# Two raw weight sets, split subtractions, powers by columns and later pages in a two-layer decoder step

## The chip, the cores and the metric

The kernel runs on one core of a Trainium2 chip. A core has TensorE (matrix products, PE in the profile, with its weight loads as PEld), VectorE (DVE), ScalarE (ACT), GpSimd (POOL) and SyncE (SP), which here only issues DMAs. The engines run their own instruction queues in order and wait for one another by semaphores. The metric is the device time of one execution in microseconds (us); lower is better.

## The reference

One inference step of a decoder with two layers, for a prompt of 512 tokens and eight samples of eight new tokens each (576 columns in all), in float32:

```python
# layer 0
h = modulate(x, norm_a, shift, scale)
qkv, z, beta_in, a_in = split(h @ w_in_a)
q, k, v = split(silu(causal_conv(qkv)))
o, s = gated_delta_rule(l2_normalize(q), l2_normalize(k), v, g, beta, s0)
x = x + gate * ((rms_norm(o) * silu(z)) @ w_out_a)
# shared keys and values
k_new, v_new = split(modulate(x, norm_kv, ...) @ w_kv)   # k: rms_norm, partial rotary
# layer 1
q, z = split(modulate(x, norm_b, ...) @ w_in_b)          # q: rms_norm, partial rotary
p = softmax(q1 @ k1) - lam * softmax(q2 @ k2)            # samples: 1024 cached positions too
x = x + gate * ((rms_norm(p @ v) * silu(z)) @ w_out_b)
```

The samples' cached keys and values stand in 128-position pages, found by a page table. Outputs are the new x, the recurrent states, the convolution states and the new keys and values.

## The kernel before

**Products in two parts.** A weight matrix is cut into sets of 1024 x 128 (512 KB). TensorE multiplies in the type fp32r, which keeps fewer bits than float32. So a set w is held as an upper part hi (w rounded to fp32r) and a lower part lo = w - hi, and the activations likewise as hhi and hlo. A product is the sum of hi x hhi, hi x hlo and lo x hhi. The 576 columns are treated in two halves of 288 (HT); a set takes 2 x 24 matmuls.

**How a set is loaded.** In the first layer (`first_parts`, `negatives`, `second_parts`, lines 919 to 943) GpSimd issues a DMA from `wall` that rounds into hi (`new_set`, L906), ScalarE writes lo = -hi (`negative`, L911), and GpSimd issues a second DMA that adds w to lo (`second_part`, L916). Sets rotate through three slots, `set0` to `set2`: two in `whi` and `wlo`, the third in the two `wraw` buffers. In the second layer (`weights`, `split_w`, lines 1971 to 2001) SP loads the raw set into `wraw` (L1979), ScalarE casts it into hi (L1994), and GpSimd subtracts in two pieces of 512 columns (L1999).

**Stages.** `Opening` computes the first modulation and the first two sets. `phase_a` runs the first layer: 47 projection tiles with eight groups (`Group`) of the recurrence woven in, then the first half of the output projection (`out_half`, sets 47 to 54). Set 55, the first of the second half, is loaded there too and used by `phase_b`. The triangular factors of a group stand in two thirds of the buffer `ckq` (three parts of 128 x 1024); group 6 uses the first and the middle one, group 7 the middle and the last. `phase_b` finishes the output projection (m = 0 to 7, two halves; `first_out` adds the residual x, loaded from `x1d` into `ch`), normalizes, and then computes eight q tiles, eight k tiles, eight v and eight z tiles, with the attention woven in. `Tile2.rows` turns a q or k tile, sums its squares, takes the power -0.5 of ten columns on GpSimd (`root`, L163), multiplies on VectorE (L2260), turns it back and frees the banks (L2268, L2271); `rotary` does four GpSimd operations on it. `Pages.loads` (L2444 to L2460) loads the samples' pages into five buffers `pg`, one of which first holds the sums of squares; GpSimd copies a page number, SP reads it and issues the load.

**The order.** No instruction chooses its place at run time. `Weave` plans on the host: every step is a generator that yields its engine, its cost in us and its conditions (`Room` is a free buffer). The planner takes the step that could start first, by rank among equals, and the order in which steps come out is the order in each engine's queue. [...] A condition orders the plan alone; real waits come from the data. `Second`, the planner of `phase_b`, fixes SP's order as well. When the plan of the first layer sees TensorE idle for more than 0.6 us, `fill` (L288) puts matmuls of no use there. Costs are constants such as `POW = 1.2`, `act(n)`, `dve(n)` (0.16 + 0.00108 n) and `pool_op(n)` (0.16 + 0.0022 n).

Of the kernel before, what the change touches and what calls it, by code (L numbers as in the profile page):

```python
# [10 lines left out]
F32 = mybir.dt.float32  # L11
# [15 lines left out]
G = 8  # L27
# [127 lines left out]

class Ctx:
    pass


def root(K, pool, x, n, tag):  # L160
# [262 lines left out]
class Opening(Weave):  # L423
# [95 lines left out]
    def sums(self):  # L519

        K, nc = self.K, self.K.nc
        nt = 5
        for k, b in ((0, 2), (4, 5), (6, 7)):
            yield "E", None, ("sum", k, b), *((Room("pt"),) if k == 0 else ())
            if k == 0:
                pt, = self.took
                ps = K.pt.tile([128, 512], F32, name="pt")
            t = self.tiles[k]
            for c in range(nt):
                K.mm(out=ps[:, c:c + 1], lhsT=t[:, 128 * c:128 * c + 128], rhs=K.ones[:, 0:1], start=(k == c == 0),  # L530
                     stop=(k == 6 and c == nt - 1))
        ms = K.small.tile([128, nt], F32, name="nms")
        yield "D", 0.55
        nc.vector.tensor_scalar(out=ms[:], in0=ps[:, 0:nt], scalar1=1.0 / D, scalar2=EPS, op0=ALU.mult, op1=ALU.add)
        self.leave(pt)
        yield "Q", POW
        r = root(K, K.small, ms[:], nt, "rn")
        yield "E", None, ("con", 0)
        self.r = [p.tile([128, 512], F32, name=n) for p, n in ((K.pa, "pa"), (K.ps, "ps"))]
        for c in range(nt):  # L540
            n = min(128, NT - 128 * c)
            for half in range(2):
                a, b = max(128 * c, half * HT), min(128 * c + n, half * HT + HT)
                if a < b:
                    K.mm(out=self.r[half][:, a - half * HT:b - half * HT], lhsT=r[:, c:c + 1].to_broadcast([128, 128]),
                         rhs=K.ident[:, a - 128 * c:b - 128 * c], start=True, stop=True)
        self.bank = self.r[1]
        self.set("r")
# [234 lines left out]
def phase_a(K, A, ctx, opening):  # L783
    tc = K.tc
    A.rows = ctx.enter_context(tc.tile_pool(name="rows", bufs=1))
    c = load_con(K, A.rows, K.con_in, "mask", "smaskb")
    K.mask = c("mask")
    K.smask = c("smask")
    K.xinit = c("xinit")
    K.strict = c("strict")  # L790
    K.half = c("half")
    K.smaskb = c("smaskb", 96)
    A.tok = A.rows.tile([128, 5, 128], F32, name="tok")
    A.ngc = A.rows.tile([128, 5, 16], F32, name="ngc")
    A.neg = A.rows.tile([128, 5, 16], F32, name="neg")
    W = Weave(K)

    for name, bufs, roomy in (("u", UB, 1), ("y", YB, 1), ("v", VB, 1), ("z", ZB, 1), ("ss", SSB, 1), ("araw", 1, 1), ("cso", KQS, 1),
                              ("kq", 2, 0), ("kt", 2, 0), ("vr", 4, 0), ("vsm", 2, 0), ("adsb", 1, 0), ("ln", 1, 0),
                              ("gb", 2, 0), ("eg", 4, 0), ("o", 1, 0), ("sm", 2, 0), ("ch", 1, 0), ("st", 2, 0), ("sa", 1, 0)):  # L800
        setattr(A, name, ctx.enter_context(tc.tile_pool(name=name, bufs=bufs)))
        if roomy:
            W.room(name, bufs)
    for name, bufs in (("scr", 2), ("set0", 1), ("set1", 1), ("set2", 1), ("pp", 2), ("pt", 2), ("pc", 1), ("po", 1), ("pa", 1), ("ps", 1)):
        W.room(name, bufs)

    for name in ("pp", "pp", "pc", "po"):
        W.taken[name] += 1
    end = opening.free["E"]
    W.free = {e: max(0.0, t - end) for e, t in opening.free.items()}  # L810
    for j in range(len(K.early)):
        for a, b in (("early", "hi"), ("full", "w")):
            W.done[(b, j)] = max(0.0, opening.done[(a, j)][0] - end), None
    A.ckq = A.rows.tile([128, 3, 8, 128], F32, name="ckq")
    A.XC = A.ln.tile([128, 2, 8, 16], F32, name="XC")
    A.WC = A.ln.tile([128, 8, 32], F32, name="WC")
    for name in ("C", "O", "gdn", "S", "masks", "post", "prep2", "inv", "ws", "eg", "vs"):
        for g in range(-3, 0):
            W.done[(name, g)] = 0.0, None
    groups = [Group(K, A, W, g) for g in range(G)]  # L820
    n = len(TILES) + 8
    W.add(1, gate_mask(K, A, W))
    W.add(1, gates(K, A, W, opening.chunks[0]))
    W.banks = opening.chunks[0]
    W.sets = {}
    W.add(-10, first_parts(K, W, n + 1))
    W.add(-1, negatives(K, W, n + 1))
    W.add(12, second_parts(K, W, n + 1))
    W.add(2, groups[0].open(0))
    W.add(2, groups[0].first(0, opening.chunks[1], (("pc", 0), ("po", 0))))  # L830
    for s in groups:
        for rank, work in ((0, s.decays()), (4, s.prep()), (6, s.inverse()), (-10, s.chunks()), (5, s.sample()), (9, s.post())):
            W.add(10 * s.g + 10 + rank, work)
    W.add(300, ada_loads(K, W, A))
    W.add(3, ada_units(K, W, A))
    W.add(1000, projections(K, A, W, groups))
    W.drive()
    K.mm = K.nc.tensor.matmul
    K.wnext += n + 1
    K.wq.append(W.sets[n][:2])  # L840
    W.last = n
    return W
# [37 lines left out]
LATER_AT = 3  # L880
SB = 3
SPARE = 1.4
POW = 1.2
HELD = 4
EV = 3
CH = 3
# [43 lines left out]
def negatives(K, W, n):  # L930
    for j in range(len(K.early), n):
        yield "A", 1.05, ("hi", j)
        negative(K, *W.sets[j][:2])
        W.set("neg", j)


def second_parts(K, W, n):
    for j, src in enumerate(sources(K, n)):
        if j >= len(K.early):
            yield "Q", 0.9, ("neg", j)  # L940
            second_part(K, W.sets[j][1], src)
            W.load("P", 3.3, "w", j)


def weave_proj(K, W, j, evac, heads=None, slots=None, halves=(0, 1)):
# [71 lines left out]
class Group:  # L1017
# [196 lines left out]
    def prep(self):  # L1214
# [40 lines left out]
        yield "S", 0.2  # L1255
        ksum = A.sm.tile([128, 5], F32, name="ksum")
        nc.vector.tensor_scalar_add(out=ksum[:], in0=ssk[:], scalar1=4 * EPS)
        yield "Q", POW
        rk = root(K, A.sm, ksum[:], 5, "rs")
        yield "S", 0.78  # L1260
        vs = self.vs = A.sm.tile([128, 5], F32, name="vs")
# [203 lines left out]
    def post(self):  # L1465

        K, A, W, g = self.K, self.A, self.W, self.g
        nc = K.nc
        last = g == G - 1
        yield "S", 0.4, ("O", g), ("gdn", g), ("ssq", g), ("sq", g)  # L1470
        x = A.sm.tile([128, 9], F32, name="ox")
        nc.vector.scalar_tensor_tensor(out=x[:, 0:8].rearrange("p (c h) -> p c h", h=2), in0=self.oms[:], scalar=1.0 / 128,
                                       in1=self.ssq[:, 0:4].unsqueeze(2).to_broadcast([128, 4, 2]), op0=ALU.mult, op1=ALU.add)
        nc.vector.scalar_tensor_tensor(out=x[:, 8:9], in0=self.oms2[:], scalar=1.0 / 128, in1=self.ssq[:, 4:5],
                                       op0=ALU.mult, op1=ALU.add)
        yield "Q", POW
        self.rs = root(K, A.sm, x[:], 9, "ro")
        W.add(10 * g + 9, self.sample_head())
        for hh in range(2):
            W.add(10 * g + 9, self.head(hh))  # L1480
        yield None, 0, ("og", g, 0), ("og", g, 1)
        W.set("post", g)
# [480 lines left out]
def dve(n):  # L1963
    return 0.16 + 0.00108 * n


def pool_op(n):
    return 0.16 + 0.0022 * n
# [18 lines left out]
def split_w(W, K, j, raw, rr, room, slot):  # L1987
    nc = K.nc
    yield "A", act(1024), ("raw", j), Room(room), *((("wa", j - 1),) if j - 1 in W.sets and j > 1 else ())
    took, = W.took  # L1990
    phi, plo = slot(took[1])
    hi = phi.tile([128, 8, 128], F32R, name="whi")
    lo = plo.tile([128, 8, 128], F32R, name="wlo")
    nc.scalar.copy(out=hi[:], in_=raw[:])  # L1994
    W.sets[j] = hi, lo, took
    W.set("wa", j)
    for q in range(0, 8, 4):
        yield "P", pool_op(512)
        nc.gpsimd.tensor_sub(out=lo[:, q:q + 4], in0=raw[:, q:q + 4], in1=hi[:, q:q + 4].bitcast(F32))  # L1999
    W.leave(rr)  # L2000
    W.set("w", j)

# [62 lines left out]
def second_norm(W, K, half):  # L2065
# [9 lines left out]
    yield "D", 0.25  # L2075
    ms = P.ss.tile([128, 3], F32, name="nms")
    nc.vector.tensor_scalar(out=ms[:], in0=ps[:, HT:HT + 3], scalar1=1.0 / D, scalar2=EPS, op0=ALU.mult, op1=ALU.add)
    yield "Q", POW
    r = root(K, P.ss, ms[:], 3, "rn")
    yield "E", None  # L2080
    for i, c in enumerate(first):
# [105 lines left out]
class Tile2:  # L2187
# [41 lines left out]
    def rows(self):  # L2229
# [24 lines left out]
        W.leave(sr)  # L2254
        yield "S", 0.2
        nc.vector.tensor_scalar(out=ss[:], in0=ss[:], scalar1=1.0 / 64, scalar2=EPS, op0=ALU.mult, op1=ALU.add)
        yield "Q", POW
        r = root(K, P.tk, ss[:], 10, "rq")
        yield "D", 0.83, ("rot", self.kind, h)
        nc.vector.tensor_mul(out=t[:], in0=t[:], in1=r[:].unsqueeze(2).to_broadcast([128, 10, 64]))  # L2260
# [173 lines left out]
class Pages:  # L2434
# [9 lines left out]
    def loads(self):  # L2444
        W, K, P = self.W, self.K, self.W.P
        nc = K.nc
        for kind, b in self.order:
            for pg in range(NPG):
                yield "Q", 0.2, Room("pg"), ("ptt",)
                i = b * NPG + pg  # L2450
                t = K.pg.tile([128, 8, 128], F32, name="pg")
                e = t[0:1, 0, 0:1].bitcast(I32)
# [136 lines left out]
def samples_end(W, K):  # L2589
# [22 lines left out]
    ms = K.small.tile([128, 5], F32, name="nms")  # L2612
    nc.vector.tensor_scalar(out=ms[:, 0:4], in0=pm[:, 0:4], scalar1=1.0 / 128, scalar2=EPS, op0=ALU.mult, op1=ALU.add)
    W.leave(xr)
    yield "Q", POW
    r = root(K, K.small, ms[:, 0:4], 4, "rn")
    yield "E", None, Room("px")
    xr, = W.took
# [27 lines left out]
class Prompt2:  # L2646
# [81 lines left out]
    def finish(self, h):  # L2728
# [13 lines left out]
        nc.vector.scalar_tensor_tensor(out=x[:], in0=ls[:, :, 0], scalar=EPS, in1=ls[:, :, 0], op0=ALU.mult, op1=ALU.mult)  # L2742
        nc.vector.scalar_tensor_tensor(out=x[:], in0=ms[:], scalar=1.0 / 128, in1=x[:], op0=ALU.mult, op1=ALU.add)
        W.leave(lr)
        yield "Q", POW
        r = root(K, P.ss, x[:], 4, "ra")
        yield "D", 0.7
        nc.vector.tensor_mul(out=o, in0=o, in1=r[:].unsqueeze(2).to_broadcast([128, 4, 128]))
# [434 lines left out]
```

## Time and profile before

| what | us |
|---|---|
| median of 3 runs | 1188.38 (1187.9 to 1188.45) |
| profiled execution | 1185.3 |
| its span, first to last instruction | 1183.3 |
| TensorE busy in it | 1145.0 |
| ScalarE, VectorE busy | 689.8, 685.8 |
| GpSimd busy | 453.5 |

The mean granted clock of TensorE is 0.997 of full speed. The profile divides the span into 40 slices; each digit is the busy share of an engine in tenths:

```profile
PE   8999999999999999999999989989999999999998
DVE  4567885867868675756643646473333446554342
POOL 3433424233334343232221442689844223232341
DMA  9796666767667475676878786322678899897143
```

A slice is 29.6 us. The first layer fills slices 1 to 22, the second half of its output projection reaches into slice 24, the q and k tiles follow up to slice 30 (there GpSimd's digits are highest and DMA's lowest), and the cached pages are read from slice 28 to 37. Matmuls are pipelined, so that a TensorE digit of 9 can hide gaps; the number of matmuls in a stretch is the better measure. In groups of instructions "out<-in" names the tiles, "x" is the count, then follow busy us, mean ns of one, the idle time before them and what ended it.

### The profile page before, as it was taken

The page shows a single profiled execution, that of the slowest core. Times are in us where ns is not written, and L with a number is a line of the kernel's source. Part 1 is how long each engine was busy: PE and PEld are TensorE (multiplying, and loading weights), DVE is VectorE, ACT ScalarE, POOL GpSimd, SP SyncE. Part 2 cuts the span into 40 slices and gives each one's busy share as a digit, 9 for nine tenths or more (in the row PEclk, how much of TensorE's full clock was granted, in tenths as well). Part 3 has the DMA queues.
Part 4 walks back from the last instruction along what each step waited for, and adds up shares of the span by engine and source line. Part 5 has one row for each costly group of instructions (what it writes and reads, how often), then busy time and mean ns, then how long its engine had stood idle before and what let it go on. Part 6 is the DMA issues. An engine that isn't in the chain of part 4 may idle for free.

```text
span 1183.3 us, 32811 instructions
## 1 busy us (share of the span) xinstructions
PE 1145.0 (97%) x12827; PEld 1048.3 (89%) x12827; DVE 685.8 (58%) x1727; ACT 689.8 (58%) x1893; POOL 453.5 (38%) x765
## 2 busy tenths in 40 slices
PE   8999999999999999999999989989999999999998
PEld 6899898998989898898999989988998878777998
DVE  4567885867868675756643646473333446554342
ACT  4666868677767877676643234765444556555320
POOL 3433424233334343232221442689844223232341
PEclk9999999999999999999999999999999999999999
DMA  9796666767667475676878786322678899897143
GB/s 371 195 234 157 156 188 146 187 147 187 165 148 204 107 208 132 204 181 183 246 183 256 281 286 248 90 72 65 225 270 286 316 302 307 312 326 272 60 128 117
DMA packets 87931, 241.03 MB, mean 204 GB/s; under 512 B 14482, under 2 KB 28690, under 8 KB 87778
## 3 DMA queue, kind: packets, MB, share of 16 engines
q1 hardware_dynamic: 71650, 180.22, 44.9%
q0 software_dynamic: 16128, 58.73, 23.0%
q8 instruction: 101, 1.65, 0.6%
q14 instruction: 52, 0.43, 0.1%
HBM read 213.07 MB, written 25.84 MB: 202 GB/s over the span
## 4 chain that ended last, share of the span: by engine, by line
PE 69%; DMA 10%; ACT 7%; POOL 5%; DVE 5%; issue 4%; SPq 0%; POOLq 0%; DVEq 0%; ACTq 0%
PE pp L267 20%; PE pp L1903 8%; PE pc L267 7%; PE pq L1903 6%; PE px L1903 6%; PE sc L1903 3%; PE po L1903 3%; PE pt L1903 3%; DMA whi<-wall 3%; PE pa L267 3%; DMA araw<-ada 2%; PE pv L1903 2%; PE pt L1908 2%; PE pt L267 2%; DMA wraw<-wall 2%
## 5 line engine op out<-in xcount | busy, mean ns | idle before, releaser
L267 PE MATMUL pp<-hlo,whi 128*128 128x288 f32 x592 | 171.1, 310 | 0.0
L1999 POOL TENSOR_TENSOR wlo<-wraw,whi 128x512 fp32r<-128x512 f32 x94 | 126.1, 1361 | 99.2 <-ACT whi L1994 88.6
L267 PE MATMUL pp<-hhi,whi 128*128 128x288 f32 x592 | 162.1, 294 | 0.0
L1903 PE MATMUL pp<-hhi,whi 128*128 128x288 f32 x432 | 133.7, 310 | 3.1 <-DVE x L1802 3.1
L1903 PE MATMUL pp<-hlo,whi 128*128 128x288 f32 x432 | 127.9, 297 | 0.0
L1903 PE MATMUL pp<-hhi,wlo 128*128 128x288 f32 x432 | 126.2, 296 | 0.0
L267 PE MATMUL pp<-hhi,wraw 128*128 128x288 f32 x576 | 124.0, 299 | 0.0
L267 PEld LDWEIGHTS pp<-hlo,whi 128*128 128x128 f32 x592 | 111.5, 188 | 1.8 <-issue 1.0
L267 PEld LDWEIGHTS pp<-hhi,whi 128*128 128x128 f32 x592 | 111.6, 189 | 0.5
L267 PE MATMUL pp<-hhi,wlo 128*128 128x288 f32 x592 | 104.6, 304 | 0.0
L267 PEld LDWEIGHTS pp<-hhi,wraw 128*128 128x128 f32 x576 | 94.2, 189 | 0.9 <-issue 0.4
L1903 PEld LDWEIGHTS pp<-hhi,whi 128*128 128x128 f32 x432 | 82.1, 190 | 7.2 <-issue 6.9
L2453 POOL COPY pg<-ptt 1x1 int32<-1x1 int32 x128 | 28.6, 230 | 153.7 <-PE px L1903 60.2
L267 PEld LDWEIGHTS pp<-hhi,wlo 128*128 128x128 f32 x592 | 85.4, 189 | 1.4 <-issue 0.8
L1107 DVE SCALAR_TENSOR_TENSOR y<-u,vec,y 128x600 f32<-128x600 f32 x96 | 80.6, 839 | 9.0 <-ACT y L1104 8.1
L267 PE MATMUL pp<-hlo,wraw 128*128 128x288 f32 x288 | 85.3, 317 | 0.0
L1903 PEld LDWEIGHTS pp<-hlo,whi 128*128 128x128 f32 x432 | 82.2, 190 | 0.0
L1903 PEld LDWEIGHTS pp<-hhi,wlo 128*128 128x128 f32 x432 | 81.4, 190 | 0.0
L916 POOL DMA_DIRECT2D wlo<-wall x38 | 34.2, 901 | 106.6 <-ACT wlo L911 67.2
L1994 ACT CAST whi<-wraw 128x1024 fp32r<-128x1024 f32 x47 | 49.0, 1047 | 31.0 <-DMA wraw<-wall 12.1
L1903 PE MATMUL pq<-hhi,whi 128*128 128x288 f32 x192 | 62.0, 323 | 1.4 <-DVE x L2205 1.0
L1903 PE MATMUL pq<-hhi,wlo 128*128 128x288 f32 x192 | 56.6, 295 | 0.0
(481 smaller groups left out, 3136.2 us busy)
## 6 DMA issues: line engine op xcount, KB each, us to landing
pg<-ck SPq DMA_DIRECT2D x64, 512.0 KB, 5.2
pg<-cv SPq DMA_DIRECT2D x64, 512.0 KB, 5.3
wraw<-wall SPq DMA_DIRECT2D x49, 512.0 KB, 5.1
whi<-wall POOLq DMA_DIRECT2D x38, 512.0 KB, 5.6
wlo<-wall POOLq DMA_DIRECT2D x38, 512.0 KB, 5.8
wraw<-wall POOLq DMA_DIRECT2D x36, 512.0 KB, 5.9
araw<-ada SPq DMA_DIRECT2D x24, 512.0 KB, 4.3
araw<-ada SPq DMA_DIRECT2D x8, 1024.0 KB, 17.3
```

The source lines that it names most:

```text
L267: return self.K.nc.tensor.matmul(**kw)
L916: K.nc.gpsimd.dma_start(out=lo[:], in_=src, accum_op=ALU.add)
L1107: nc.vector.scalar_tensor_tensor(out=y[:, :YW], in0=u[:, j:j + YW], scalar=cw[j], in1=y[:, :YW], op0=ALU.mult, op1=ALU.add)
L1903: return self.K.nc.tensor.matmul(**kw)
L1908: return self.K.nc.tensor.transpose(**kw)
L1994: nc.scalar.copy(out=hi[:], in_=raw[:])
L1999: nc.gpsimd.tensor_sub(out=lo[:, q:q + 4], in0=raw[:, q:q + 4], in1=hi[:, q:q + 4].bitcast(F32))
L2453: nc.gpsimd.tensor_copy(out=e, in_=P.ptt[0:1, i:i + 1])
```

## The change

Four edits:

1. `first_parts`, `negatives` and `second_parts` end at set 53. Sets 54 and 55 go by a new generator: SP loads the raw set into the first third of `ckq` once group 6's outputs are done, or into the middle third once group 7's inverse is done; ScalarE copies it to hi when its slot is free; GpSimd subtracts in two pieces.
2. In `split_w`, of sets 8 to 19 of the second layer (the q tiles and the first four k tiles) VectorE subtracts the second piece.
3. The plan's cost of a power is 0.5 + 0.15 us per column, in place of 1.2 us for each. The instruction itself is the same.
4. In the plan, pages are loaded only after the last square of the output projection's result ("sq", 1, 7).

```diff
+def power_op(n):
+    return 0.5 + 0.15 * n
...
-        yield "Q", POW
+        yield "Q", power_op(nt)
         r = root(K, K.small, ms[:], nt, "rn")
...
-    W.add(-10, first_parts(K, W, n + 1))
-    W.add(-1, negatives(K, W, n + 1))
-    W.add(12, second_parts(K, W, n + 1))
+    W.add(-10, first_parts(K, W, n - 1))
+    W.add(-1, negatives(K, W, n - 1))
+    W.add(12, second_parts(K, W, n - 1))
+    for j, at, free in ((n - 1, 0, ("O", G - 2)), (n, 1, ("inv", G - 1))):
+        W.add(12, direct_set(K, A, W, j, sources(K, n + 1)[j], at, free))
...
-POW = 1.2
+HALF = 8, 20
+PAGES_AT = 1, 7
...
+def direct_set(K, A, W, j, src, at, free):
+
+    yield None, 0, free
+    raw = A.ckq[:, at]
+    K.nc.sync.dma_start(out=raw, in_=src)
+    W.load("S", 1.5, "raw", j)
+    yield "A", 1.05, ("raw", j), ("w", j - 3), Room(f"set{j % 3}")
+    hi, lo = (p.tile([128, 8, 128], F32R, name=n) for p, n in ((K.whi, "whi"), (K.wlo, "wlo")))
+    W.sets[j] = hi, lo, W.took[0]
+    K.nc.scalar.copy(out=hi[:], in_=raw)
+    W.set("hi", j)
+    for q in range(0, 8, 4):
+        yield "P", 1.29
+        K.nc.gpsimd.tensor_sub(out=lo[:, q:q + 4], in0=raw[:, q:q + 4], in1=hi[:, q:q + 4].bitcast(F32))
+    W.set("w", j)
...
     for q in range(0, 8, 4):
-        yield "P", pool_op(512)
-        nc.gpsimd.tensor_sub(out=lo[:, q:q + 4], in0=raw[:, q:q + 4], in1=hi[:, q:q + 4].bitcast(F32))
+        shared = q and HALF[0] <= j < HALF[1]
+        yield ("S", dve(512)) if shared else ("P", pool_op(512))
+        (nc.vector if shared else nc.gpsimd).tensor_sub(out=lo[:, q:q + 4], in0=raw[:, q:q + 4], in1=hi[:, q:q + 4].bitcast(F32))
...
-                yield "Q", 0.2, Room("pg"), ("ptt",)
+                yield "Q", 0.2, Room("pg"), ("ptt",), ("sq", *PAGES_AT)
```

The other powers get their own counts in the same way: 5 and 9 columns for each group of the first layer, 3 for each half of the second norm, 10 for a q or k row, 4 for the samples' norm and for each head.

More of the change, by code (lines that the diff above doesn't have):

```diff
@@ L1257, in prep @@
         nc.vector.tensor_scalar_add(out=ksum[:], in0=ssk[:], scalar1=4 * EPS)
-        yield "Q", POW
+        yield "Q", power_op(5)
         rk = root(K, A.sm, ksum[:], 5, "rs")
@@ L1475, in post @@
                                        op0=ALU.mult, op1=ALU.add)
-        yield "Q", POW
+        yield "Q", power_op(9)
         self.rs = root(K, A.sm, x[:], 9, "ro")
@@ L2077, in second_norm @@
     nc.vector.tensor_scalar(out=ms[:], in0=ps[:, HT:HT + 3], scalar1=1.0 / D, scalar2=EPS, op0=ALU.mult, op1=ALU.add)
-    yield "Q", POW
+    yield "Q", power_op(3)
     r = root(K, P.ss, ms[:], 3, "rn")
@@ L2256, in rows @@
         nc.vector.tensor_scalar(out=ss[:], in0=ss[:], scalar1=1.0 / 64, scalar2=EPS, op0=ALU.mult, op1=ALU.add)
-        yield "Q", POW
+        yield "Q", power_op(10)
         r = root(K, P.tk, ss[:], 10, "rq")
@@ L2614, in samples_end @@
     W.leave(xr)
-    yield "Q", POW
+    yield "Q", power_op(4)
     r = root(K, K.small, ms[:, 0:4], 4, "rn")
@@ L2744, in finish @@
         W.leave(lr)
-        yield "Q", POW
+        yield "Q", power_op(4)
         r = root(K, P.ss, x[:], 4, "ra")
```

## The prediction

> **What bounds the kernel now.** I read the page first. TensorE is busy for 97% of the span, and in its chain of work that ended last TensorE holds 69%; so a change gains only where TensorE stands still, runs at a lower clock or does filler work. The columns are busy time, share and count; then the chain's shares by engine.
>
> ```profile
> span 1183.3 us, 32811 instructions
> PE 1145.0 (97%) x12827; PEld 1048.3 (89%) x12827; DVE 685.8 (58%) x1727; ACT 689.8 (58%) x1893; POOL 453.5 (38%) x765
> PE 69%; DMA 10%; ACT 7%; POOL 5%; DVE 5%; issue 4%; SPq 0%; POOLq 0%; DVEq 0%; ACTq 0%
> ```
>
> Next, TensorE's waits (total, times, longest), the matmuls in order of time around the end of the first layer, and the busy times by stretch (each engine's busy us with its count, then the granted clock, DMA share and GB/s). They show three places that the change touches.
>
> ```profile
> PE pt L1908 <- DVE qT L2271: 3.2, 3, 1.7
> PE pp L1903 <- DVE x L1802: 3.1, 1, 3.1
> PE pt L1908 <- DVE qkt L2260: 2.7, 6, 1.2
> ...
> 640.43 0.29 PE L267 MATMUL pp<-hhi,whi 128*128 128x288 f32 x1
> 641.13 3.80 PE L288 MATMUL pp<-cT,con_ident 128*128 128x224 bf16 x38 [0.41 <-DVE rst L1806]
> 644.70 0.38 PE L267 MATMUL pp<-hhi,wlo 128*128 128x288 f32 x1
> ...
> 682.80:690.50 7.70, 4.61 (x24) 4.40 (x23) 2.56 (x7) 2.10 (x4) 3.05 (x3) 0.78 1.03 390
> 687.10:690.50 3.40, 3.40 (x17) 3.40 (x16) 1.59 (x6) 1.41 (x3) 2.52 (x2) 0.50 1.03 382
> ...
> 757.00:776.00 19.00, 19.00 (x148) 19.00 (x147) 9.76 (x10) 16.61 (x28) 18.84 (x19) 1.00 0.28 85
> 776.00:800.00 24.00, 19.85 (x148) 18.53 (x147) 18.74 (x32) 14.06 (x34) 19.99 (x23) 1.00 0.22 66
> 800.00:826.00 26.00, 24.29 (x237) 23.31 (x236) 10.55 (x17) 15.17 (x28) 25.42 (x31) 1.00 0.22 62
> ```
>
> At 641 TensorE runs 38 fillers while the first layer's last set but one lacks its lower part. At 683 it waits 3.1 us and then has half the clock, with the DMA engines full (1.03). From 776 to 826 it loses 4.15 + 1.71 = 5.9 us, with GpSimd busy 45 of 50 us. One matmul of 288 columns takes 0.133 us (46 in 6.12, below).
>
> **Part 1, the last two sets raw.** Rows: the chain of work, then GpSimd in order of time, then the page's groups and DMA issues.
>
> ```profile
> 644.93 6.12 PE pp L267 x46
> ...
> 627.09 0.85 POOL L906 DMA_DIRECT2D whi<-wall  x1
> 633.32 0.54 POOL L906 DMA_DIRECT2D whi<-wall  x1 [5.38 <-PE pp L267]
> 635.59 0.88 POOL L916 DMA_DIRECT2D wlo<-wall  x1 [1.73 <-ACT wlo L911]
> ...
> L1999 POOL TENSOR_TENSOR wlo<-wraw,whi 128x512 fp32r<-128x512 f32 x94 | 126.1, 1361 | 99.2 <-ACT whi L1994 88.6
> L1994 ACT CAST whi<-wraw 128x1024 fp32r<-128x1024 f32 x47 | 49.0, 1047 | 31.0 <-DMA wraw<-wall 12.1
> wraw<-wall SPq DMA_DIRECT2D x49, 512.0 KB, 5.1
> wlo<-wall POOLq DMA_DIRECT2D x38, 512.0 KB, 5.8
> ...
> L267 PE MATMUL pa<-XA,ckq x32: 218/218/267, 526.4 to 594.3; 64*64 64x64 f32 x32
> ```
>
> Today a set's upper part is loaded when its buffer comes free (set 54 at 627.09, set 55 at 633.32), negated by ScalarE, and the lower part is added by a second transfer: set 54's is issued at 635.59 and there at 635.59 + 5.8 = 641.4. TensorE wants it at 640.43 + 0.13 = 640.56, and does the matmul at 644.70: **4.1 us** lost, 0.8 of them a true wait and 3.3 filler laid too long by the plan. After the change the raw set is there long before (the middle third of ckq is last read at 594.3, plus 5.1 for the load). From 627.09 on there remain a copy of 1.05 and two subtractions of 1.36: ready about 631.5 with handovers, 9 us before use. So no filler. Hidden: ScalarE's copy replaces the negation of the same length; GpSimd gets 4 x 1.36 for four issues, and starts nothing between 627.9 and 633.3; the two loads on SP's queue replace four on GpSimd's. SP may stand at the second one until 594.3, with residual inputs queued behind it, of which u holds four ahead; set 55's buffer comes free only 39 us later. Bounds: 0 (if the next stage takes it back, below) to 4.1. I take 4.1, since all that opens the next stage hangs on this set.
>
> **Part 2, the pages later.** SP's issues in order of time, the chain, a cast of ScalarE, the modulation's weight loads, and a stretch behind the projection.
>
> ```profile
> 672.71 0.36 SPq L2458 DMA_DIRECT2D pg<-ck  x1
> 675.85 0.36 SPq L2458 DMA_DIRECT2D pg<-ck  x1
> 677.55 0.35 SPq L2458 DMA_DIRECT2D pg<-ck  x1
> 678.00 0.38 SPq L2060 DMA_DIRECT2D ch<-x1d  x1
> 678.49 0.37 SPq L1979 DMA_DIRECT2D wraw<-wall  x1
> 679.72 0.34 SPq L2458 DMA_DIRECT2D pg<-ck  x1
> ...
> 678.00 7.47 DMA ch<-x1d
> ...
> 686.86 1.05 ACT L1994 CAST whi<-wraw 128x1024 fp32r<-128x1024 f32 x1 [0.24 <-DMA wraw<-wall]
> L1903 PEld LDWEIGHTS pt<-kT,cT x192: 106/110/111, 701.3 to 746.4; 128*32 128x32 f32 x192
> 701.00:747.00 46.00, 46.00 (x591) 43.10 (x590) 30.61 (x69) 20.62 (x43) 12.43 (x11) 1.00 0.61 209
> ```
>
> Three pages of 512 KB were issued just ahead of the small load that the chain waits for, which takes 7.47 us. At 390 GB/s a page is 1.34 us, so without them it lands 4.0 us sooner, more than the 3.1 us wait. With the wait goes the half clock: 17 matmuls in 3.4 us, two of which began before; 3.4 - 15 x 0.133 = 1.4 us. Together 4.5 and, by starts, 0.2 of handover: 4.7. What is late next is the weight set behind the same pages: cast at 686.86, less 4.0 = 682.9, plus 1.05 and two subtractions of 1.26 to 1.36, is ready at 686.6; TensorE would want it 24 matmuls after 682.8, at 686.0. That gives 0.6 to 0.8 back: **3.9 us**, between 2 and 4.7. The later place costs nothing: after the projection DMA is 0.61 busy for 46 us, so 18 us are free for 5.4 us of pages, and no page is read before the eighth q row's power, well after 763.7 (row below). The new condition orders queues only; SP gets no new semaphore. Behind the pages on SP come the last modulation loads; their matmuls go on until 746.4, so they have time.
>
> **Part 3, halves to VectorE, and powers at their own length.** Groups between 757 and 826, then VectorE's groups at 640 to 660, and the power's line.
>
> ```profile
> L1999 POOL TENSOR_TENSOR wlo<-wraw,whi 128x512 fp32r<-128x512 f32 x19 | 27.3, 1455 | 4.6 <-ACT whi L1994 4.5
> L2174 DVE TENSOR_TENSOR hlo<-kT,hhi 128x512 fp32r<-128x512 f32 x1 | 0.7, 679 | 0.0
> ...
> L1531 DVE TENSOR_TENSOR hlo<-z,hhi 128x288 fp32r<-128x288 f32 x4 | 5.9, 1541 | 0.0
> L1828 DVE TENSOR_TENSOR hlo<-scr,hhi 128x288 fp32r<-128x288 f32 x4 | 1.7, 460 | 0.0
> ...
> L163 POOL TENSOR_TENSOR rqy<-qss,power x16: 1953/1961/2099, 763.7 to 869.0; 128x10 f32<-128x10 f32 x16
> ```
>
> Twelve halves move, some nine of them between 757 and 826: GpSimd sheds 9 x 1.46 = 13 of 64 busy us in 69. VectorE gets 9 x 0.68 = 6 on top of 39, alone. Beside a GpSimd subtraction the same VectorE operation grew from 0.46 to 1.54, so a half may cost up to 0.68 + 1.08 = 1.76. In 800 to 826 VectorE has room, and I take back all 1.7. In 776 to 800 it is already 18.7 of 24 busy, and three or four halves at 0.7 to 1.8 could fill it; I take half of 4.15. Start to start these gaps are 1.4 us larger, as a matmul's modelled end covers part of them; half of that, 0.7. Sum **4.5 us**, bounds 0 and 7.3. Powers take the time they took (0.5 + 0.15n gives 2.0 for the row's 1.96 at ten columns, where the plan had 1.2), so only orders move, in both layers: 0, bounds plus or minus 3 (one break with its clock, below).
>
> [...]
>
> **Sum.** 4.1 + 3.9 + 4.5 = 12.5 us. Against the profiled execution, 1185.3 (span 1183.3 and 2.0 around it), that is 1172.8. The median of the runs, 1188.38, lies 3.1 above the profiled execution; the same saving from it gives **1175.9 us**.
>
> **Rivals.**
>
> 1. The transfers of the second layer's output projection are its bound (share 1.03 between 682.8 and 690.5). Then parts 1 and 2 don't add: what counts is the 4 x 1.34 = 5.4 us of transfers taken out, of which TensorE can gain 4.7. With part 3: 9.2, so 1179. For it: the full DMA. Against it: by the waits TensorE lost 3.1 us to transfers in the whole stage, and behind it DMA is at 0.61. Chance 0.15.
> 2. The re-laid first layer. For it: every power of nine columns is 1.85 - 1.2 = 0.65 longer in the plan, and all behind it shifts; today there is one such break:
>
> ```profile
> 458.70:465.30 6.60, 5.14 (x37) 4.46 (x36) 4.99 (x13) 5.76 (x20) 4.12 (x8) 0.74 0.64 124
> 461.80:465.30 3.50, 3.50 (x18) 3.13 (x17) 3.36 (x11) 2.73 (x12) 1.89 (x6) 0.51 0.92 215
> ```
>
>    It is 1.5 us idle and some 1.4 of half clock: 2.9 us. Two more of them: 1181.7, chance 0.10. One fewer, with part 3 in full: 12.5 + 2.9 + 2.8 gives 1170, chance 0.10.
> 3. The halves gain nothing, VectorE being held by GpSimd: 8.0 us, 1180.4, chance 0.10.
> 4. [...] In 757 to 826 VectorE's queue is in order, and the banks' release (L2271) stands in it. If all twelve halves take 1.76 and TensorE waits for each, 21.1 us are lost against 8.0 gained: 1201. It decides from six halves on (10.6). Against it: VectorE idles 30 of these 69 us. Chance 0.05.
> 5. The change does not do what it says: a filler remains, as the plan still sees the set late; 1180, inside the range; 0.04.
>
> [...]
>
> **Numbers.** Forecast 0.46, between 1173 and 1179; rivals as given. The range 1169.5 to 1183.0 reaches to rivals 1, 2, 3 and 5; rival 4 and the spread about each leave out 0.2. A measurement of this kernel tells 0.2% (2.4 us) from no change: faster 0.89, same 0.06 (the upper ends of rivals 1 to 3), slower 0.05 (rival 4).
>
> **What would show it.** Part 1: no fillers before the layer's end, and the first L1903 matmul some 4 us sooner. Part 2: no wait for x L1802 and no half clock in the projection; perhaps a short one for wlo. Part 3: GpSimd clearly below full between the q rows, waits for L2271 and L2260 under 3 us in sum; if VectorE is full there instead, rival 3. A new half-clock row before 640 would be rival 2. The forecast is wrong if the stages' starts move but not the end.

## The result: faster, and by more than forecast

| | before | changed kernel |
|---|---|---|
| median of the runs (us) | 1188.41 (1187.9 to 1188.52) | 1168.69 (1167.18 to 1170.36) |
| ratio of the times | 1 | 0.9837 (0.9818 to 0.9856) |
| profiled execution, its span | 1185.3, 1183.3 | 1167.18, 1165.4 |
| first matmul of the second layer | 650.9 | 641.6 |
| from there to the end of the span | 532.4 | 523.8 |

The forecast was 1175.9, with a range from 1169.5 to 1183.0. The time lies 0.8 us below the range. Of the 17.9 us by which the span is shorter, 9.3 were gained before the second layer's first matmul and 8.6 behind it. The forecast had 4.1 for the first and 3.9 + 4.5 = 8.4 for the second. So in these two traces the second layer came out near what was worked out, and about 5.2 us of the first layer's gain were not foreseen. The median lies 7.2 us below the forecast, while the spans give 17.9 - 12.5 = 5.4. The other 1.8 come from the medians: the profiled execution was 3.1 us below its median before and is only 1.5 below it now.

The rows of the second layer's first products, before and changed (least, middle and longest duration in ns; first and last start in us):

```profile
L1903 PE MATMUL pp<-hhi,whi x432: 289/296/442, 650.9 to 895.9; 128*128 128x288 f32 x144
```

```profile
L1927 PE MATMUL pp<-hhi,whi x432: 289/296/404, 641.6 to 877.3; 128*128 128x288 f32 x144
```

The lead is 9.3 us at their first start and 18.6 at their last, at the end of the q and k tiles. In between, the modulation's first weight load moved from 701.3 to 688.5, a lead of 12.8 us. So the output projection gave 3.5 us and the q and k tiles 5.8; 0.7 of it was lost again behind them.

First the page of the changed kernel: busy time, share and count, then the shares of the chain that ended last.

```profile
span 1165.4 us, 32715 instructions
...
PE 1133.8 (97%) x12771; PEld 1041.2 (89%) x12771; DVE 689.2 (59%) x1739; ACT 688.4 (59%) x1893; POOL 436.4 (37%) x753
...
PE 78%; ACT 6%; DMA 6%; DVE 3%; issue 3%; POOL 2%; SPq 0%; POOLq 0%; ACTq 0%; DVEq 0%
```

TensorE holds more of that chain than before: its share of the chain rose from 69% to 78%, while DMA fell from 10% to 6% and GpSimd from 5% to 2%. It executes 56 instructions fewer. These are fillers (55 of them) and one record; the line of `fill` shows it, in the kernel before and in the changed one (the count stands behind the x):

```profile
L288 PE MATMUL pp<-cT,con_ident x79: 256/259/269, 46.2 to 644.7; 128*128 128x224 bf16 x79
```

```profile
L292 PE MATMUL pp<-cT,con_ident x24: 256/259/269, 45.3 to 630.8; 128*128 128x224 bf16 x24
```

The last filler now runs at 630.8, and only four are left after 99 us; the 38 at 641 are gone, and so are 21 at 573 to 576, of which the forecast said nothing.

TensorE's waits in the changed kernel from 640 to 740 (line, total, times, longest), then by stretch of the second layer (busy us and count of PE, PEld, DVE, ACT, POOL; granted clock; DMA share; GB/s):

```profile
PE pp L1927 <- DVE rst L1830: 0.7, 1, 0.7
PE pp L1927 <- ACT whi L2018: 0.4, 1, 0.4
PE pt L1927 <- ACT scr L2876: 0.3, 1, 0.3
```

```profile
641.00:660.00 19.00, 19.00 (x193) 18.28 (x192) 10.26 (x22) 6.89 (x13) 8.93 (x9) 1.00 0.77 269
660.00:680.00 20.00, 18.90 (x142) 18.50 (x141) 12.77 (x31) 5.76 (x10) 8.70 (x8) 1.00 0.96 340
680.00:703.00 23.00, 23.00 (x248) 21.91 (x247) 17.00 (x38) 10.31 (x20) 8.67 (x10) 1.00 0.81 262
755.00:790.00 35.00, 34.43 (x270) 34.21 (x269) 23.65 (x42) 25.42 (x55) 27.45 (x33) 1.00 0.22 67
790.00:825.00 35.00, 34.45 (x314) 33.31 (x314) 15.91 (x21) 17.98 (x33) 33.72 (x42) 1.00 0.37 112
```

The wait of 3.1 us for x and the half clock behind it (0.50 from 687.1 to 690.5 before, 1.00 in all these stretches) are gone from the output projection; a wait of 0.4 us for a weight set (whi) came, and one of 0.7 for the residual's addition (rst). Between the query rows TensorE loses 70.00 - 68.88 = 1.1 us where it lost 5.9. The one wait left there, and the twelve subtractions that VectorE took over:

```profile
PE pt L1932 <- DVE qkt L2285: 1.1, 3, 0.6
```

```profile
L2024 DVE TENSOR_TENSOR wlo<-wraw,whi x12: 677/693/1781, 692.6 to 779.1; 128x512 fp32r<-128x512 f32 x12
```

A half costs VectorE 0.68 us alone and up to 1.78 us, close to the two bounds that the prediction had put on it (0.68 and 1.76). One of its signs was only half there: GpSimd has fallen to 78% busy from 755 to 790, but from 790 to 825 it is still at 96%.

### The profile page after: what moved, and what is told of

Same layout as the page of the kernel before. It is cut to its first block, busy times and chain, and to the rows that moved or that the text cites. A ratio compares the mean times of both kernels' runs of the same rounds, so it can differ in the third digit from the quotient of the medians.

```text
span 1165.4 us, 32715 instructions
## 1 busy us (share of the span) xinstructions
PE 1133.8 (97%) x12771; PEld 1041.2 (89%) x12771; DVE 689.2 (59%) x1739; ACT 688.4 (59%) x1893; POOL 436.4 (37%) x753
## 4 chain that ended last, share of the span: by engine, by line
PE 78%; ACT 6%; DMA 6%; DVE 3%; issue 3%; POOL 2%; SPq 0%; POOLq 0%; ACTq 0%; DVEq 0%
PE pp L271 23%; PE pp L1927 13%; PE pc L271 7%; PE px L1927 5%; PE pq L1927 5%; PE pt L1927 3%; PE pa L271 3%; PE sc L1927 3%; PE pt L271 3%; PE pt L1932 3%; PE po L1927 3%; DMA wraw<-wall 2%; PE pv L1927 2%; DMA whi<-wall 2%; PE ps L271 2%
## 5 line engine op out<-in xcount | busy, mean ns | idle before, releaser
L2024 POOL TENSOR_TENSOR wlo<-wraw,whi 128x512 fp32r<-128x512 f32 x82 | 109.7, 1354 | 113.1 <-ACT whi L2018 94.9
L1927 PE MATMUL pq<-hhi,whi 128*128 128x288 f32 x184 | 58.9, 320 | 1.0 <-DVE x L2230 1.0
L271 PEld LDWEIGHTS pp<-hlo,wraw 128*128 128x128 f32 x288 | 54.6, 189 | 1.7 <-issue 1.0
```

Source lines behind the costliest of these rows:

```text
L271: return self.K.nc.tensor.matmul(**kw)
L1927: return self.K.nc.tensor.matmul(**kw)
L2024: (nc.vector if shared else nc.gpsimd).tensor_sub(out=lo[:, q:q + 4], in0=raw[:, q:q + 4], in1=hi[:, q:q + 4].bitcast(F32))
```

## The experiments

In all traces "start" is the first matmul of the second layer and "rest" the span from there on. The rows behind the starts are those of the second layer's matmuls; the starts of four kernels as an example (first and last start in us):

```profile
L1922 PE MATMUL pp<-hhi,whi x432: 289/296/577, 647.8 to 893.4; 128*128 128x288 f32 x144
```

```profile
L1907 PE MATMUL pp<-hhi,whi x432: 289/296/442, 647.8 to 889.0; 128*128 128x288 f32 x144
```

```profile
L1927 PE MATMUL pp<-hhi,whi x432: 289/296/407, 651.4 to 880.6; 128*128 128x288 f32 x144
```

```profile
L1928 PE MATMUL pp<-hhi,whi x432: 289/296/403, 639.5 to 868.9; 128*128 128x288 f32 x144
```

They belong to raw_alone, powers_alone, no_powers and all_five of the table. Medians are of three to ten runs, the ratio is to the kernel before on the same chip. One profile is one execution, and not always one near the median: that of powers_alone took 1187.1 us, that of halves_alone 1191.2, each the longest of its runs.

| kernel | raw sets | halves | later pages | price of a power | start | rest | median | ratio (95% interval) |
|---|---|---|---|---|---|---|---|---|
| before | | | | 1.2 | 650.9 | 532.4 | 1188.4 | 1 |
| powers_alone | | | | 0.50 + 0.15n | 647.8 | 537.4 | 1182.3 | 0.9954 (0.9937 to 0.9970) |
| raw_alone | x | | | 1.2 | 647.8 | 534.7 | 1186.3 | 0.9997 (0.9979 to 1.0015) |
| pages_alone | | | x | 1.2 | 652.5 | 528.6 | 1181.2 | 0.9956 (0.9937 to 0.9975) |
| halves_alone | | x | | 1.2 | 650.8 | 538.3 | 1187.4 | 0.9996 (0.9977 to 1.0015) |
| no_powers | x | x | x | 1.2 | 651.4 | 529.2 | 1179.9 | 0.9915 (0.9887 to 0.9944) |
| no_raw | | x | x | 0.50 + 0.15n | 645.4 | 522.6 | 1171.3 | 0.9872 (0.9837 to 0.9907) |
| no_pages | x | x | | 0.50 + 0.15n | 640.1 | 531.8 | 1171.7 | 0.9856 (0.9834 to 0.9879) |
| no_halves | x | | x | 0.50 + 0.15n | 641.3 | 531.6 | 1173.9 | 0.9873 (0.9842 to 0.9905) |
| changed | x | x | x | 0.50 + 0.15n | 641.6 | 523.8 | 1168.7 | 0.9837 (0.9818 to 0.9856) |
| all_first | x | x | x | first layer 0.50 + 0.15n | 640.8 | 524.0 | 1168.2 | 0.9840 (0.9789 to 0.9890) |
| all_second | x | x | x | second layer 0.50 + 0.15n | 651.5 | 523.5 | 1177.8 | 0.9914 (0.9885 to 0.9943) |
| all_near | x | x | x | 0.56 + 0.15n | 646.4 | 526.1 | 1173.3 | 0.9852 (0.9800 to 0.9904) |
| all_near3 | x | x | x | 0.53 + 0.15n | 646.0 | 525.2 | 1172.7 | 0.9891 (0.9857 to 0.9925) |
| all_near2 | x | x | x | 0.44 + 0.15n | 643.0 | 523.1 | 1170.6 | 0.9870 (0.9846 to 0.9895) |
| all_low | x | x | x | 0.6 | 647.8 | 538.2 | 1188.4 | 1.0002 (0.9979 to 1.0025) |
| all_nine | x | x | x | 0.50 + 0.15n at n = 9, else 1.2 | 646.0 | 525.3 | 1176.2 | 0.9918 (0.9892 to 0.9943) |
| all_five | x | x | x | 0.50 + 0.15n at n = 5, else 1.2 | 639.5 | 528.4 | 1170.5 | 0.9891 (0.9832 to 0.9951) |
| best | x | x | x | 1.2 at n = 9, else 0.50 + 0.15n | 639.5 | 521.9 | 1166.5 | 0.9811 (0.9785 to 0.9837) |
| again | x | x | x | 0.50 + 0.15n | 639.5 | 525.1 | 1166.9 | 0.9823 (0.9795 to 0.9851) |

How far may one trace's start be trusted? Several kernels have the same order of TensorE's matmuls in the first layer, fillers left out, so that their starts can be compared:

| the same first layer | starts |
|---|---|
| before, pages_alone, halves_alone | 650.8 to 652.5 |
| raw_alone, no_powers, all_second | 647.8 to 651.5 |
| powers_alone, no_raw | 645.4 and 647.8 |
| changed, again, no_pages, no_halves, all_first | 639.5 to 641.6 |
| all_five, best | 639.5 and 639.5 |

So one order's start is repeated to within 2 to 4 us, and the prices move it by more: third row against first by 3.0 to 7.1 us, fourth against second by 6.2 to 12.0.

### Each part by itself

**powers_alone.** Only the costs in the plan change (in it "Q" and "P" stand for GpSimd, "S" and "D" for VectorE):

```diff
-        yield "Q", POW
+        yield "Q", power_op(n)      # at all seven places; n columns
```

> The plan's power costs alone (0.5 + 0.15 us per column), nothing else of the change; the instructions are the same, only orders move. Theory 'chance' (the prediction's): the re-laid first layer gains nothing on average, the first matmul of the second layer stays within 3 us of 650.9, and the time within 3 us of 1188.4. Theory 'accuracy': most of the first layer's unforeseen 5 us come from the nine-column powers being planned at their true length: the second layer starts near 645.5 to 646.5 (before its last sets' fillers, which stay), and the time is 1182 to 1184.

Measured: 1182.3 us, ratio 0.9954, the time of the theory of accuracy. A change in which no useful instruction differs, only the order, gains 0.3 to 0.6%. The start came 3.1 us earlier, less than that theory had said, and TensorE's 21 fillers at 573 were gone.

**raw_alone.** Only sets 54 and 55 go by `direct_set`:

```diff
-    W.add(-10, first_parts(K, W, n + 1))
+    W.add(-10, first_parts(K, W, n - 1))
...
+        W.add(12, direct_set(K, A, W, j, sources(K, n + 1)[j], at, free))
```

> The last two sets of the first layer raw, nothing else. Prediction: no filler before the last set but one, the second layer starts at 650.9 - 4.1 = 646.8, and all of it reaches the end: 1184.3. Rival 'transfers': the second layer's output projection is bound by its transfers, the start moves but the end does not: 1187 to 1188.

Measured: no difference, 0.9997 (0.9979 to 1.0015), though the 38 fillers are gone and the start is 3.1 us earlier in its trace. The rest is 2.3 us longer. Its second layer has the order of before, matmul for matmul, and runs 3 us ahead of it up to 840 us; from 1050 us on 0.6 to 1.0 of that is left. TensorE's waits for the pages' transfers from 860 to 1110 are 1.6 + 1.5 us, against 0.3 + 0.7 before, and these 2.1 us are most of the loss:

```profile
PE po L1922 <- DMA pg<-cv: 1.6, 3, 0.6
PE px L1922 <- DMA pg<-ck: 1.5, 2, 0.9
```

```profile
PE px L1903 <- DMA pg<-ck: 0.7, 1, 0.7
...
PE po L1903 <- DMA pg<-cv: 0.3, 1, 0.3
```

**pages_alone.** One condition in the plan:

```diff
-                yield "Q", 0.2, Room("pg"), ("ptt",)
+                yield "Q", 0.2, Room("pg"), ("ptt",), ("sq", *PAGES_AT)
```

> The pages behind the output projection, nothing else. Prediction: the wait of 3.1 us for x L1802 near 683 and its half clock go, 0.6 to 0.8 us come back as a wait for a weight set: 1184.5, bounds 1183.7 and 1186.4. Rival: the wait only moves to another load (the weight sets are as late): 1187 to 1189.

Measured: 1181.2 us, 0.9956 (0.9937 to 0.9975). The rest is 3.8 us shorter, where the prediction had 3.9 for this part: no wait for x and no half clock in the projection. From 640 to 690 TensorE is busy 49.59 us at full clock, against 46.51 at 0.97 in the kernel before. The rows are the kernel before, then pages_alone:

```profile
640.00:690.00 50.00, 46.51 (x397) 45.28 (x396) 27.26 (x63) 16.57 (x33) 16.61 (x19) 0.97 0.88 312
```

```profile
640.00:690.00 50.00, 49.59 (x431) 48.55 (x430) 30.20 (x65) 17.79 (x35) 18.60 (x17) 1.00 0.84 290
```

**halves_alone.** Twelve subtractions move to VectorE:

```diff
-        yield "P", pool_op(512)
-        nc.gpsimd.tensor_sub(...)
+        shared = q and HALF[0] <= j < HALF[1]
+        yield ("S", dve(512)) if shared else ("P", pool_op(512))
+        (nc.vector if shared else nc.gpsimd).tensor_sub(...)
```

> Half of the subtractions of sets 8 to 19 on VectorE, nothing else. Prediction: 4.5 us from the 7.3 us that TensorE loses between 776 and 826, at 1183.9; the powers' wrong length in the plan remains. Rival 'VectorE is held by GpSimd': no gain, 1187 to 1189, and VectorE over 90% busy in 776 to 800. Rival 'the powers were the cause of the waits, not the subtractions': 1186 or more here, and the gain shows only with the powers' costs.

Measured: no difference, 0.9996 (0.9977 to 1.0015). From 740 to 840 TensorE's waits for the rows fell from 5.9 to 3.8 us only; later the pages' transfers were late (waits from 860 to 1110):

```profile
PE pt L1909 <- DVE qkt L2262: 3.8, 4, 1.4
```

```profile
PE px L1904 <- DMA pg<-ck: 3.7, 2, 2.0
PE po L1904 <- DMA pg<-cv: 1.8, 3, 1.3
```

What follows from the four: alone they give about 5.5, 0.4, 5.2 and 0.5 us (one minus the ratio, times 1188), 11.6 in all, where the change gives 19.4. Each of these is known to some 2 us, the sum to some 4. So together the parts give more than by themselves.

### Each part undone in the changed kernel

Here the same four diffs are taken out of the changed kernel, one in each run.

> The changed kernel with one thing undone: the plan counts every power at 1.2 us again. Theory 1 (each part keeps in the full change what its own stage shows, and the powers are the 5 us of the first layer that the prediction lacked): the second layer's first matmul at about 646.5 instead of 641.6, the stages behind as in the changed kernel, 1173 to 1175 us. Theory 2 (the parts simply add as they did alone: powers -4.5, raw -0.5, pages -5.5, halves 0 from about 1187.5): 1181 to 1182. Theory 3 (the halves and the powers need each other, because with the powers' old price the order of the query rows stays wrong): the waits for the rows' roots and transposes between 740 and 830 come back by 3 us or more, 1176 to 1179.

> The changed kernel with weight sets 54 and 55 split ahead again. Theory 1: 38 fillers come back before the second layer's first matmul, which moves from 641.6 to about 645.5, and the time to about 1172.5 (+4). Theory 2 (parts add as alone, raw -0.5): no measurable difference, 1169. A third way, as raw alone showed it: the start is 4 us later and half of that is made up in the stretch of the pages.

> The changed kernel with the first pages not held behind the output projection. Theory 1 and theory 2 agree on the sign: the wait of 3 to 5 us for x and the half clock behind it come back near 674, 1172.5 to 1174. They differ if it is under 1170: then the pages cost the projection nothing once the rest is changed.

> The changed kernel with all lower parts of the rows back on GpSimd. Theory 1: waits for the rows' roots and transposes of 4 to 6 us between 740 and 830, 1173 (+4.5). Theory 2 (halves 0 as alone): 1168.7, no difference, because the powers' truer price has put the rows right already. Theory 3 (needs both): 1173 or more, with the query rows waiting as in the kernel before.

Measured, as differences of the ratios to the changed kernel's 0.9837 times 1188: powers 9.3, raw sets 4.2, halves 4.3, pages 2.3 us. Both intervals taken together, each is known to some 4 us either way. So by the times only the powers' share is clear of nothing; for the other three the traces have to speak. Without raw sets the start is 645.4, as the first theory had it. Without the later pages the wait and the clock come back:

```profile
PE pp L1927 <- DVE x L1826: 3.3, 1, 3.3
```

```profile
671.90:683.00 11.10, 7.82 (x40) 7.62 (x39) 4.22 (x10) 3.87 (x6) 4.47 (x5) 0.69 0.97 334
```

The third theory (powers and halves need each other) is seen in the waits between the query rows. They are 5.9 us with neither part (before), 3.8 with the halves alone, 5.2 with the prices alone (no_halves), and 1.1 with both. The rows of no_powers (one) and no_halves (three):

```profile
PE pt L1932 <- DVE qkt L2285: 3.8, 4, 1.4
```

```profile
PE pt L1932 <- DVE qkt L2284: 3.8, 5, 1.8
PE pp L1927 <- ACT ch L2239: 1.0, 2, 0.5
PE pt L1932 <- DVE qT L2295: 0.4, 1, 0.4
```

The larger part stands before the start: 651.4 without the prices, 641.6 with them. Behind it the rests differ by 5.4 us: these 2.7 us of waits, and waits for pages from 860 to 1110 us, which are 5.4 us in no_powers and 2.0 in the changed kernel. In sum that is more than 9.3, as the profiled execution of no_powers took 2.5 us more than its median and that of the changed kernel 1.5 less.

### In which layer the price counts

```diff
 # all_first: power_op(n) at the first layer's three places, POW at the second's four
 # all_second: the other way round
```

> The changed kernel, but the powers' prices by columns stand in the first layer's plan alone; the second layer's stay at 1.2 us. Theory 3 (in the second layer the prices and the halves need each other): the second layer starts near 641 as in the changed kernel, and takes some 525 us instead of 519, since its order is then that of no_powers: 1173 to 1176 us. Rival (the prices matter to the first layer alone): 1169, as the changed kernel.

> The changed kernel, but the prices by columns stand in the second layer's plan alone. Theory 3: the second layer starts at 648 to 651 as in no_powers and raw_alone, and takes 519 us as in the changed kernel: 1174 to 1178 us. Rival (the first layer's later start is made up in the stretch of the pages, since transfers bound that): under 1172.

Measured: 1168.2 and 1177.8 us. With the prices in the first layer alone the time is that of the changed kernel; with those in the second layer alone it is that of no_powers (0.9914 and 0.9915). So the first layer is where most of the prices' gain lies. The third theory, as far as it promised 5 us for the second layer, is not borne out: the 2.7 us of waits that the prices take out there do not show in these times, of which that of all_first has an interval of 6 us to either side.

That the second layer's prices are worth nothing is not shown either. With the halves, later pages and 1.2 us in the second layer (no_powers, all_first, all_five, all_nine: one order of its matmuls) the rest is 524.0 to 529.2 us, on average 526.7; with the prices by columns (changed, again, no_raw, best, all_second: one order too) it is 521.9 to 525.1, on average 523.4. The difference of 3.3 us is near the 2.7 us of waits, but the two ranges overlap. The times disagree: all_five and best, which have the same first layer, differ by 4.0 us in their medians, and the two pairs above by none.

### Is the price right, or only another one?

The trace shows what a power takes. Rows of the kernel before: columns n in the shape, least, middle and longest duration.

```profile
L163 POOL TENSOR_TENSOR rsy<-ksum,power x8: 1196/1200/2032, 90.6 to 525.9; 128x5 f32<-128x5 f32 x8
L163 POOL TENSOR_TENSOR roy<-ox,power x8: 1822/1834/1975, 166.0 to 621.5; 128x9 f32<-128x9 f32 x8
```

At nine columns 1.2 was 0.63 too low; at five columns the new 1.25 is no better than the old 1.2.

```diff
 def power_op(n):
-    return 0.5 + 0.15 * n
+    return 0.56 + 0.15 * n                          # all_near
+    return 0.53 + 0.15 * n                          # all_near3
+    return 0.44 + 0.15 * n                          # all_near2
+    return 0.6                                      # all_low
+    return 0.5 + 0.15 * n if n == 9 else 1.2        # all_nine
+    return 0.5 + 0.15 * n if n == 5 else 1.2        # all_five
```

> The changed kernel with every power 0.06 us dearer in the plan (0.56 + 0.15 a column instead of 0.50 + 0.15). Theory 4 (the price helps because it is near what a power takes, 1.20 us at five columns and 1.83 at nine): 1167 to 1172, the order being nearly as good. Theory 5 (a changed price only deals the list scheduler another hand, and the change's hand was a good one): any time from 1168 to 1180, most likely above 1173, with the second layer's start anywhere from 641 to 650.

> The changed kernel with every power at 0.6 us in the plan, half to a third of what it takes. Theory 4: worse than at 1.2 us (no_powers, 1180): the matmuls that wait for a nine-column power's result are placed 1.2 us too early, and the gaps before them grow; 1180 to 1186, second layer's start at 650 or later. Theory 5: like any other hand, 1172 to 1182, and it may well beat no_powers.

> The changed kernel with the price by columns for the nine-column power alone (1.85 us, once for each group of the first layer); all others at 1.2 us. Theory 4 (truth of the price): the five-column powers' 1.25 differs from 1.2 by less than the scatter of their durations, so this is the whole effect: first layer as in the changed kernel, second layer's start 641 to 643, 1167 to 1172 us. Theory 5 (another hand): any start from 641 to 651, 1168 to 1180 us.

> The changed kernel with the price by columns for the five-column powers alone (1.25 us instead of 1.2; one in the opening and one for each group of the first layer). Theory 4: a price that changes by 0.05 us does nothing: start 648 to 651 and 1176 to 1181 us, as without the prices. Theory 5: any start from 641 to 651; if it is under 645, a twentieth of a microsecond deals as good a hand as the whole edit.

> The changed kernel with every power 0.06 us cheaper in the plan (0.44 + 0.15 a column: 1.19 at five, 1.79 at nine). Theory 4: start 641 to 643, 1167 to 1172 us. Theory 5: start anywhere from 641 to 651, most likely 645 to 649 as with 0.06 us dearer, 1170 to 1180 us.

> The changed kernel with every power 0.03 us dearer in the plan (0.53 + 0.15 a column). Theory 4: start 641 to 643, 1167 to 1172 us. Theory 5: start anywhere from 641 to 651, 1168 to 1180 us.

Measured: 0.03 or 0.06 us more on every power moves the start from 641 to 646. The nine-column price, the one that was wrong, gives 646.0 by itself; the five-column price, changed by 0.05, gives 639.5. The fourth theory (truth of the price) expected the opposite of these last two, in the times as well (1176.2 and 1170.5 us), and as the whole account it fell, although all_near2 came as it said (643.0, 1170.6). Nor do the two add: they start 5.4 and 11.9 us ahead of the 651.4 of no_powers, and both together, in the changed kernel, 9.8. By the ratios neither alone is told from no_powers (0.9918 and 0.9891 against 0.9915).

One part of it can be placed. The opening has one power of five columns. Wherever the plan has 1.25 us or more for it, the first filler stands at 44.4 to 45.4 (first number behind the durations); at 1.2 or less, at 46.2 to 46.8, and once at 50.9 (all_second):

```profile
L292 PE MATMUL pp<-cT,con_ident x54: 256/259/269, 44.8 to 568.8; 128*128 128x224 bf16 x54
```

```profile
L292 PE MATMUL pp<-cT,con_ident x66: 256/259/269, 46.6 to 569.2; 128*128 128x224 bf16 x66
```

The first row is all_five (1.25), the second all_near2 (1.19): 1.8 us for 0.06 us of price.

all_low is worse in the second layer, not in the first: its start is no later than raw_alone's, but its rest of 538.2 is 14 us longer than that of the changed kernel, with waits of 6.9 us between 740 and 840:

```profile
PE pt L1933 <- DVE qkt L2286: 3.7, 3, 2.6
PE px L1928 <- POOL qs L2503: 1.2, 1, 1.2
PE pt L1933 <- ACT whi L2019: 1.0, 1, 1.0
PE pp L1928 <- ACT ch L2241: 1.0, 2, 0.5
```

So near the truth a changed price deals another order. That the price does harm because it is so far from the truth, or that this one order is a bad one, can't be told apart by one kernel.

### The best pieces put together

```diff
 def power_op(n):
-    return 0.5 + 0.15 * n
+    return 1.2 if n == 9 else 0.5 + 0.15 * n        # best
```

> The changed kernel with the nine-column power at 1.2 us in the plan, all others by columns: the first layer's order of all_five, the second layer's of the changed kernel. If price truth counts for nothing and the two layers' orders keep what they gave: second layer's start 639 to 640, 519 to 521 us from there, 1 to 3 us below the changed kernel on the same chip. If truth counts: above it by 2 us or more, the nine-column power being the one that was 0.65 us off.

> The changed kernel once more, beside the one above on the same chip: 1167 to 1171 us, second layer's start 640 to 642.

Measured on one chip: 1166.47 (1162.28 to 1167.59) and 1166.87 (1164.39 to 1171.65). The kernel with the wrong nine-column price is as fast as the changed one, so the rightness of that price is worth nothing that can be measured. A faster version than the changed kernel was not shown.

## Why the prediction was right, and where it failed

**Part 1 (4.1 us): right in the changed kernel, but not by itself.** Of the 38 fillers before the layer's end four are left, at 630.5. Undoing it there moves the start from 641.6 to 645.4, and costs 4.2 us by the ratios, with an interval that reaches to nothing. In the kernel before the same edit was worth nothing: by its trace, waits for the pages' transfers took the gain back. The prediction's lower bound, 0, was that case, though it had looked for it in the next stage and not 200 to 400 us later.

**Part 2 (3.9 us): right.** The wait for x and the half clock are gone, and a wait of 0.4 us for a weight set came back where 0.6 to 0.8 were expected. Alone it gave 3.8 us in the trace and 5.2 by the ratio; undone in the changed kernel it cost 2.3 by the ratio, give or take some 4.

**Part 3 (4.5 us): the size was right, its cause only half.** The waits between the rows went from 5.9 to 1.1 us, below the 3 that the prediction had named. But the subtractions alone took 2.1 of it. The other 2.7 came only when the second layer's powers had their new prices too, which the same part had put at nothing; which of these prices did it, that of ten columns or those of three and four, no run tells. So it was in part luck that 4.5 was near. Rival 3 in its pure form (VectorE held by GpSimd) is excluded by the 0.69 us that the middle one of the twelve halves takes. Single ones took longer: the three of 1.72 to 1.78 us, in the changed kernel's trace, all began while GpSimd was subtracting. Beside a power it was not so: from 752.10 to 752.78 us a half took 0.68 us, the time of one alone, in the middle of a power that GpSimd ran from 751.30 to 753.24.

**The step that failed** is the last of part 3: "Powers take the time they took ..., so only orders move, in both layers: 0, bounds plus or minus 3 (one break with its clock, below)." That term was put at 0. No instruction became shorter, that is true; but the first layer's order became one in which TensorE reaches the second layer 6 to 12 us earlier (with raw sets, 639.5 to 641.6 against 647.8 to 651.5), and undoing the prices costs 9.3 us. Without raw sets it is 645.4 and 647.8 against 650.8 to 652.5. The bound was sized by the one break that the trace of before showed at 458. That break is still there in the changed kernel:

```profile
454.00:463.00 9.00, 7.59 (x62) 6.84 (x62) 5.95 (x14) 6.88 (x22) 4.77 (x8) 0.81 0.55 124
```

What went instead: about 1 us in the opening, two stretches of filler at 573 to 576 (21 matmuls, 2.1 us by their starts), and small gaps all through the groups. Filler is no measure of the gain, though: all_five has 34 at 565 to 569 and starts as early as any. A smaller share of the miss, 1.8 of 7.2 us, is in the sum, which took a saving worked out on one profiled execution from the median of the runs. Rival 2's better branch (1170) was nearest in time and had the right cause, the re-laid first layer, with the wrong place. What the bound should have been is shown by the starts in the table: with raw sets, from 639.5 to 651.5 us.

What stays open is why the one order is better than the other beyond these places. Of the orders with raw sets, all six whose prices go by columns, wholly or in part, start at 646.4 or earlier, and those with 1.2 or 0.6 throughout the first layer at 647.8 or later. These are six orders against two. So a truer price may help on average; single cases don't show it, and more orders would have to be tried.

## What to carry to other kernels

Where a planner on the host lays out the queues, a change of any cost in it deals a new order, and the gain or loss of that is to be bounded by the spread of other orders (here some 12 us in the second layer's start, and 1166 to 1188 us in the times of the kernels with all other parts), not by the one break that the present order shows. Run one order more than once before one trace's start is read: here it varied by 2 to 4 us. Tell such a gain from that of the edit itself by undoing parts in the full change as well as by making them alone: four parts that gave 11.6 us singly gave 19.4 together. Time won in one stage can be lost to the transfers of a later one: raw_alone came 3.1 us ahead and lost 2.3 of them, most of it in waits for pages.

## What the runs showed of the hardware

**Behind one gap the granted clock fell to half for 3.4 us or longer, and not each time.** The same gap stands at 452 to 455 us in six traces, ahead of the same instruction. The rows are the first matmul behind it, with the idle time ahead of it, and the clock of the 9 to 11 us from there on (the number before the DMA share). First the changed kernel (its stretch is quoted above, 0.81), then no_raw, no_halves and no_pages, two fences each:

```profile
455.67 1.14 PE L271 MATMUL pa<-XA,ckq 64*64 64x64 f32 x16 [1.41 <-ACT WF L1657]
```

```profile
455.51 1.14 PE L271 MATMUL pa<-XA,ckq 64*64 64x64 f32 x16 [1.44 <-ACT WF L1639]
```

```profile
453.70:463.00 9.30, 7.75 (x72) 6.89 (x72) 7.11 (x16) 7.83 (x25) 6.37 (x9) 1.00 0.53 120
```

```profile
455.49 1.14 PE L271 MATMUL pa<-XA,ckq 64*64 64x64 f32 x16 [1.87 <-ACT WF L1657]
```

```profile
453.20:463.00 9.80, 7.82 (x74) 6.96 (x73) 7.12 (x16) 8.30 (x25) 6.43 (x9) 1.00 0.50 113
```

```profile
454.05 1.14 PE L271 MATMUL pa<-XA,ckq 64*64 64x64 f32 x16 [1.78 <-ACT WF L1657]
```

```profile
452.00:463.00 11.00, 9.22 (x64) 8.43 (x63) 6.37 (x14) 7.28 (x22) 5.07 (x8) 0.69 0.45 101
```

An idle time of 1.41 us was followed by half the clock for about 3.4 us (9.00 x 0.19 x 2; from 457.20 to 460.62 us the granted clock is 0.50), one of 1.78 by about 6.8 us (11.00 x 0.31 x 2), and those of 1.44 and 1.87 by none. In again 1.88 us was followed by about 3.4 us of half clock (10.00 x 0.17 x 2), in all_first 1.72 by about 6.4 up to 463 us (10.40 x 0.31 x 2). So the length of a short gap alone doesn't decide; what does was not shown.

By an estimate from these lengths, half the clock for 3.4 or 6.8 us costs at most half of that, 1.7 or 3.4 us, and this if TensorE is the bound there. So by this estimate the clock alone can make two executions of one order differ by that much. no_powers and raw_alone, whose first layers have one order, start 3.6 us apart; how much of that is the clock was not shown.
